# Layer 1's output projection: five token tiles begun beside the last four attention heads, and the last pair's rows in one load

## The chip, the cores and the metric

The kernel runs on one core of a Trainium2 chip. Five engines work side by side, each through its own instructions in a fixed order: TensorE (PE: matrix products into PSUM), VectorE (DVE), ScalarE (ACT), GpSimd (POOL) and SyncE (SP, which here issues every DMA). The metric is the device time of one execution in microseconds (us), the median of several. Lower is better.

## What is computed

Two decoder layers over 1024 tokens of width 1024, and a final RMSNorm. Layer 0 mixes by forgetting attention, layer 1 by native sparse attention (NSA). The part that matters here is the end of layer 1: sixteen heads of width 64 make `o`, `o` is gated, and then the output projection, the residual and the norm follow.

```python
def reference(x, norm_g, fox_w_in, ..., nsa_w_out, final_g):
    for i in range(DEPTH):
        h = rmsnorm(x, norm_g[i])
        ...
        x = x + y
    return rmsnorm(x, final_g)

def nsa_mixer(h, ...):
    ...
    o = g[..., 0:1] * o_c + g[..., 1:2] * o_s + g[..., 2:3] * o_w
    return (o.reshape(B, S, W) * jax.nn.silu(z)) @ w_out
```

`o_s` is attention over chosen blocks, `o_w` over a window of 512 tokens, `o_c` over compressed blocks. `z` is a projection of `h` of the same width as `o`.

## The kernel before

**Precision.** A float32 product is made of three: each operand is split into a high part `hi` (ACT copies it) and a low part `lo` (the difference, by DVE or POOL), and `mm3` (lines 133 to 135) issues hi·hi, hi·lo and lo·hi into one PSUM sum. One such group of three has 128 channels of `o` (one value of k, eight in all), 128 tokens and 512 output columns.

**The head stage of layer 1.** `run_attn` goes through 32 half-heads: head `h` from 0 to 15, for each the later 512 tokens (`s` = 1) and then the earlier ones (`s` = 0). While the products with V of one half-head run (`O_n`, lines 1315 to 1317, after the transposes `ptp_n` on line 1307), the scores of the next are made (`S_n`, line 1275; DVE masks them and finds the extremum on line 1282, ACT takes the exponential on line 1285, POOL splits it on lines 1288 and 1289, and a transposing DMA brings it to `hT`). `finish` (lines 1347 to 1351) ends a half-head: DVE writes `u`, POOL adds it into `ot`. After the second head of a pair, `close` transposes `ot` (`ptn_n`, line 1364), DVE and POOL apply scale and gate, and SP writes 128 rows of `oF` in DRAM. Pair 7 (heads 14 and 15) writes the last 128 of the 1024 rows.

**The filler.** `merge` puts other work between the steps of the heads: for every unit of head cost that is recorded, so much filler (`ratio`, here 0.36). The filler is `nsa_zs`: eight projections `z` (48 products each, `nz`), and after each half of the last one the loading and splitting of four 128-row parts of the output weights `wo` (`load_wout`: SP loads float32 rows into `lo`, ACT copies them to `hi`, line 536, DVE subtracts, line 537). Where a generator yields a function, the filler waits until it returns true. A scheduler then orders each engine's instructions by what it expects to be ready; the order is fixed before the run.

**The output stage.** `out_layer` takes eight tiles of 128 tokens in the order 4, 5, 6, 7, 0, 1, 2, 3. For each: load the tile of `oF` into `of` (line 696), split it into `ohi` and `olo` (lines 697 and 698), make 48 products (two halves of 512 columns, eight k), load the residual `xr`, add (line 727), square and sum, and scale by the norm (line 106), and write the result out. For tiles 4 and 5, seven of the eight k are issued ahead of the loop (`early`). All of it stands behind the head stage in the program.

**Buffers.** In the head stage PSUM has two banks for `O_n`, `nz` and the like (`ps_a`), two pairs of banks for scores (`ps_s2`) and two for transposes. `out_tiles` shares its buffers with the weights of the `z` projections: one `wst` tile for what is loaded, two pairs `whi`, `wlo` for the split. K and V of head group 2 (heads 8 to 11) lie in the pool `kv[0]`, those of group 3 in the pool `at`.

Of the kernel before, what the change touches and what calls it, by code (L numbers as in the profile page):

```python
# [8 lines left out]
F32 = mybir.dt.float32  # L9
# [26 lines left out]
def f(ap):  # L36
    return ap.bitcast(F32)
# [3 lines left out]
def tile_fox_nsa(ctx, tc, a, out):  # L41
# [20 lines left out]
    def ps_a(name):  # L62
        return psA.tile([P, 512], F32, tag="A", name=name)
# [451 lines left out]
    def out_tiles(name):  # L515
        return wp.tile([P, KC, P], F32, tag="wst", bufs=1, name=f"of{name}"), *out_parts(name)
# [6 lines left out]
    def load_wout(pool, i, half):  # L523

        hi, lo = (pool.tile([P, 4, D], F32R, tag=f"h{half}{x}", name=f"wo{i}_{half}_{x}") for x in range(2))
        for k in range(4):
            r = 4 * (1 - half) + k
            dma(f(lo[:, k, :]), wD[i][r * P:(r + 1) * P, :])
        if i:
            yield 2000  # L530
        for k in range(4):
            for c in range(2):
                if i:
                    yield 400
                cs = slice(c * 512, c * 512 + 512)
                A.copy(hi[:, k, cs], f(lo[:, k, cs]))
                (V if i else G).tensor_tensor(lo[:, k, cs], f(lo[:, k, cs]), f(hi[:, k, cs]), OP.subtract)
# [138 lines left out]
    sa.release()  # L676


    def out_layer(ow, w, src, res, g, after, name, early=()):

        gB = ow.tile([P, D], F32, name=f"gB{name}")
        dma(gB, g.to_broadcast([P, D]))
        pend, first = [], list(ready.get("ys", {}))
        bufs = 4 if first else 2
        cs = [slice(half * 512, half * 512 + 512) for half in range(2)]

        def tiles(t):
            if not early:
                return out_tiles(f"{name}_{t}")
            of = ow.tile([P, KC, P], F32, tag="of", bufs=3, name=f"of{name}_{t}")  # L690
            return of, *out_parts(f"{name}_{t}")

        def products(t, tile, ys, ks):
            of, oh, ol = tile
            c = slice(ks[0], ks[-1] + 1)
            dma(of[:, c, :], src[:, t * P:(t + 1) * P].rearrange("(k p) t -> p k t", p=P)[:, c, :])
            A.copy(oh[:, c, :], of[:, c, :])  # L697
            V.tensor_tensor(ol[:, c, :], of[:, c, :], f(oh[:, c, :]), OP.subtract)  # L698
            for half, ts in enumerate(cs):
                if len(ys) <= half:  # L700
                    ys.append(ps_a(f"y{name}_{t}_{half}"))
                for k in ks:
                    wh, wl = w[k // 4]
                    mm3(ys[half], oh[:, k, :], ol[:, k, :], wh[:, k % 4, ts], wl[:, k % 4, ts], k == 0, k == KC - 1)

        begun = {}
        for t in early:
            ps = ps_s2(f"y{name}_{t}")
            begun[t] = tiles(t), [ps[:, half, :] for half in range(2)]
            for ks in (range(0, 4), range(4, 7)):  # L710
                products(t, *begun[t], ks)
        for t in (4, 5, 6, 7, 0, 1, 2, 3):
            tk = slice(t * P, (t + 1) * P)
            ys = ready.get("ys", {}).pop(t, [])
            steps = () if ys else (range(0, 4), range(4, KC)) if t == 4 else (range(KC),)
            xt = ow.tile([P, D], F32, tag="x", bufs=bufs, name=f"xr{name}_{t}")
            nm = Norm(ow, xt, f"n{name}_{t}", bufs)
            if t in begun:
                tile, ys = begun.pop(t)
                steps = (range(7, 8),)  # L720
            elif not ys:
                tile = tiles(t)
            for ks in steps:
                products(t, tile, ys, ks)
            dma(xt, res[tk, :])
            for ps, ts in zip(ys, cs):
                V.tensor_tensor(xt[:, ts], ps, xt[:, ts], OP.add)  # L727
# [495 lines left out]
    class NsaSuper:  # L1223
# [30 lines left out]
        def unit(self, y, qi):  # L1254
# [100 lines left out]
        def close(self):  # L1355
# [9 lines left out]
            V.scalar_tensor_tensor(o, pt, vinv[:, self.g:self.g + 1], o, OP.mult, OP.add)  # L1365
            G.tensor_tensor(o, o, ready["z", p, s][s], OP.mult)
            dma(oF[p * P:(p + 1) * P, s * 512:(s + 1) * 512], o)
            yield 450
# [6 lines left out]
    fo = tc.alloc_tile_pool(name="fo", bufs=1, reuse_waits="tile")  # L1375
    def after1(t, xt, h):
        for c in (slice(0, 512), slice(512, D)):
            dma(out[t * P:(t + 1) * P, c], h[:, c])
# [104 lines left out]
```

## Time and profile before

| | |
|---|---|
| median of 3 runs | 1527.96 us (1526.06 to 1528.8) |
| profiled execution | 1529.59 us, of which 1527.8 us from the first to the last instruction |
| mean granted TensorE clock | 0.974 |
| busy share of PE, DVE, ACT, POOL | 93%, 70%, 53%, 37% |
| chain that ended last, share by engine | PE 63%, DVE 16%, ACT 8%, DMA 6%, issue 4% |
| matrix products | 10488, each with one weight load |

Times in the views count from the span's start. A window view lists, for a stretch of the span, the busy time of each engine with the number of instructions that touch the stretch, then the granted TensorE clock (PEclk), the mean busy share of the 16 DMA engines and GB/s. A busy PE is not PE at its peak: products overlap, and the time from one start to the next is what counts. PEld is the weight loads. In a chain, each row is a piece of the work that ended last, with its start and length.

### The profile page before, as it was taken

How to read it: one execution, taken by the hardware profiler on the slowest of the kernel's cores; microseconds unless marked ns; L12 is line 12 of the kernel's file. 1: busy time of each engine (PE TensorE's matmuls, PEld its weight loads, DVE VectorE, ACT ScalarE, POOL GpSimd, SP SyncE). 2: the span in 40 equal slices, each digit the busy share in tenths (PEclk: the TensorE clock that was granted, in tenths of full speed). 3: DMA queues.
4: the chain of work that ended last, by engine and by line, in shares of the span. 5: the costliest groups of instructions: out<-in, count | busy, mean ns of one | idle time of the engine just before them, and what ended most of it. 6: DMA issues, size and time to landing. Idle time of an engine off the chain costs nothing.

```text
span 1527.8 us, 29541 instructions
## 1 busy us (share of the span) xinstructions
PE 1421.9 (93%) x10488; PEld 1179.8 (77%) x10488; DVE 1066.2 (70%) x2759; ACT 805.1 (53%) x2028; POOL 565.1 (37%) x604
## 2 busy tenths in 40 slices
PE   5999999999999778999999899999999999988698
PEld 4888888888788556878888777778888888876576
DVE  6586878788787864457554668677888788888143
ACT  5364646646565652224131664476767676676031
POOL 1232222222322600033333332366767766575000
PEclk9999999999999979999999998999999999999799
DMA  7796777866777765342435577586777857766442
GB/s 254 238 180 142 163 158 157 182 153 143 172 165 166 178 124 197 121 136 83 156 98 163 148 187 201 180 184 133 180 152 146 204 124 144 189 142 147 132 151 83
DMA packets 405812, 242.72 MB, mean 159 GB/s; under 512 B 332513, under 2 KB 353889, under 8 KB 405409
## 3 DMA queue, kind: packets, MB, share of 16 engines
q1 hardware_dynamic: 405664, 240.84, 64.8%
q8 instruction: 83, 1.36, 0.4%
q14 instruction: 65, 0.52, 0.1%
HBM read 120.96 MB, written 44.11 MB: 108 GB/s over the span
## 4 chain that ended last, share of the span: by engine, by line
PE 63%; DVE 16%; ACT 8%; DMA 6%; issue 4%; POOL 1%; SPq 1%; POOLq 0%; DVEq 0%; ACTq 0%
PE S_n L1275 5%; PE y L133 3%; PE y L135 3%; PE y L134 3%; PE ptp_n L1307 3%; ACT P_n L1285 2%; DVE P_n L1282 2%; PE v L133 2%; PE v L135 2%; PE v L134 2%; DVE hl L605 2%; PE S L585 2%; ACT P L603 2%; PE k L133 2%; PE k L134 2%
## 5 line engine op out<-in xcount | busy, mean ns | idle before, releaser
L1285 ACT ACTIVATE P_n<-P_n,m_n 128x640 f32<-128x640 f32 (+7 forms) x256 | 187.2, 732 | 68.5 <-DVE m_n L1282 34.4
L1275 PE MATMUL S_n<-nk,nq 128*128 128x320 f32 (+5 forms) x768 | 180.0, 350 | 8.6 <-DVE m_n L1282 8.3
L603 ACT ACTIVATE P<-P,m 128x512 f32<-128x512 f32 (+1 forms) x192 | 116.9, 610 | 131.4 <-DVE m L594 130.7
L574 POOL TENSOR_TENSOR Bd<-B,tri 128x128 f32<-128x128 f32 x128 | 62.3, 502 | 245.8 <-DVE m L594 227.5
L1289 POOL TENSOR_TENSOR hl_n<-P_n,hl_n 128x640 f16<-128x640 f32 (+4 forms) x128 | 145.0, 1133 | 9.8
L1275 PEld LDWEIGHTS S_n<-nk,nq 128*128 128x128 f32 x768 | 125.2, 193 | 20.9 <-DVE m_n L1282 10.8
L605 DVE SCALAR_TENSOR_TENSOR hl<-P,hl 128x512 f16<-128x512 f32 (+1 forms) x192 | 124.6, 667 | 20.5 <-ACT hl L604 19.5
L1282 DVE CUSTOM_DVE_ANT_0 P_n<-S_n,wmask 128x640 f32<-128x640 f32 (+2 forms) x192 | 113.4, 595 | 25.7 <-PE S_n L1275 16.0
L1288 POOL CAST hl_n<-P_n 128x640 f16<-128x640 f32 (+4 forms) x128 | 77.0, 601 | 122.1 <-ACT P_n L1285 107.8
L150 ACT ACTIVATE pth_n<-ptp_n 128x512 f16<-128x512 f32 (+1 forms) x160 | 85.9, 547 | 49.9 <-PE ptp_n L1307 48.8
L133 PE MATMUL y<-wo,ohi 128*128 128x512 f32 x240 | 97.5, 406 | 15.4 <-ACT ohi L697 13.9
L151 DVE SCALAR_TENSOR_TENSOR ptl_n<-ptp_n,pth_n 128x512 f16<-128x512 f32 (+1 forms) x160 | 99.9, 632 | 15.4 <-ACT pth_n L150 13.9
L1307 PE MATMUL ptp_n<-ident,P_n 128*128 128x128 f32 x576 | 92.4, 281 | 9.4 <-DVE ptl_n L151 4.3
L135 PE MATMUL y<-wo,olo 128*128 128x512 f32 x240 | 95.9, 402 | 0.8 <-DVE olo L698 0.8
L134 PE MATMUL y<-wo,ohi 128*128 128x512 f32 x240 | 96.0, 400 | 0.0
L604 ACT ACTIVATE hl<-P 128x512 f16<-128x512 f32 (+1 forms) x192 | 92.5, 513 | 4.5 <-DMA pT<-hl 3.1
L1307 PEld LDWEIGHTS ptp_n<-ident,P_n 128*128 128x128 f32 x576 | 66.9, 143 | 20.8 <-DVE ptl_n L151 9.5
L585 PE MATMUL S<-KH,Q 128*128 128x512 f32 (+1 forms) x192 | 68.1, 368 | 11.3 <-DVE m L594 10.9
L1315 PE MATMUL O_n<-nv,pth_n 128*128 128x64 f16 x576 | 72.0, 196 | 6.5 <-ACT pth_n L150 5.5
L727 DVE TENSOR_TENSOR xr<-y,xr 128x512 f32<-128x512 f32 x32 | 21.5, 689 | 73.5 <-PE y L135 65.6
L1315 PEld LDWEIGHTS <-pth_n 128*128 128x128 f16 x576 | 52.2, 98 | 25.3 <-ACT pth_n L150 11.1
L1316 PE MATMUL O_n<-nv,pth_n 128*128 128x64 f16 x576 | 71.0, 194 | 0.0
(384 smaller groups left out, 4566.0 us busy)
## 6 DMA issues: line engine op xcount, KB each, us to landing
nq<-qD SPq DMA_DIRECT2D x64, 256.0 KB
B<-cD SPq DMA_DIRECT2D x16, 512.0 KB
wo<-wD SPq DMA_DIRECT2D x16, 512.0 KB
nq<-qD SPq DMA_DIRECT2D x64, 128.0 KB
of<-oF SPq DMA_DIRECT2D x11, 512.0 KB
x<-in_x_dram SPq DMA_DIRECT2D x8, 512.0 KB
wst_k<-in_fox_w_dram SPq DMA_DIRECT2D x8, 512.0 KB
wst_v<-in_fox_w_dram SPq DMA_DIRECT2D x8, 512.0 KB
```

Of the source, the lines that this page charges most:

```text
L133: T.matmul(ps, wh, mh, start=first, stop=False, **kw)
L134: T.matmul(ps, wh, ml, start=False, stop=False, **kw)
L135: T.matmul(ps, wl, mh, start=False, stop=last, **kw)
L151: V.scalar_tensor_tensor(lo[:, 0:n], pt[:, 0:n], scale, h, OP.mult, OP.subtract)
L603: A.activation(L[:, 0:n], L[:, 0:n], AF.Exp, bias=init, scale=-1.0, accum_out=self.lr[:, col + c:col + c + 1])
L605: V.scalar_tensor_tensor(lo[:, cs], L[:, 0:n], UP, hi[:, cs], OP.mult, OP.subtract)
L1275: T.matmul(ps[:, b, 0:w], self.q[x][:, qi * P:(qi + 1) * P], k[:, k0 + b * w:k0 + b * w + w], start=(x == 0), stop=(x == 1))
L1282: V.tensor_tensor_reduce(dst, src, mk, 1.0, 3e38, OP.add, OP.min, m)
L1285: A.activation(L, L, AF.Exp, bias=m, scale=-1.0, accum_out=self.l[:, y, qi:qi + 1])
L1289: G.tensor_tensor(hl[:, n:2 * n], L, hl[:, 0:n], OP.subtract)
L1307: T.transpose(pt[:, (x + i) * P:(x + i + 1) * P], L[:, kb * P - k0:(kb + 1) * P - k0], ident)
L1315: T.matmul(o, hi, v[:, 0:64], start=first, stop=False)
```

## The change

- `out_start` is new filler behind the last `z` projection. It makes products of the output projection from rows of `oF` that are already written: for tiles 4, 5 and 6 first k = 0 to 3, then k = 4 to 6, and for tiles 7 and 0 k = 0 to 6 in one piece.
- The sums of tiles 4, 5 and 6 are taken out of PSUM after each piece: their residual rows are loaded early into the space of K and V of head group 2 (`xs1`), and DVE adds each piece there. Tiles 7 and 0 keep their sums in the two pairs of score banks (`ys1`), and so wait until the last scores are made (`"scores"`).
- From super 24 on (head 12, later half) the filler's ratio is 0.62; before that it is 0.35 and not 0.36.
- The loads of the output weights' first half are issued ahead of the second half of the last `z` projection; their split, and all of the second half, come after it. Half of the subtractions of the split go to POOL.
- Behind the heads, `out_rest` loads the last pair's 128 rows of `oF` for all tokens (in two halves, `l7`), splits them once, and makes the products of k = 7 for the five begun tiles from them (6 each). Tiles 1, 2 and 3 are made whole as before. Layer 0's call of `out_layer` is left with the parts that it used.

```diff
-    def run_attn(supers, lead, late):
+    def run_attn(supers, lead, late, ratios):
...
         for n, sup in enumerate(supers):
+            if n in ratios:
+                yield (ratios[n],)
...
         if i:
-            yield 2000
+            yield 0
...
-                (V if i else G).tensor_tensor(lo[:, k, cs], f(lo[:, k, cs]), f(hi[:, k, cs]), OP.subtract)
+                (V if i and c else G).tensor_tensor(lo[:, k, cs], f(lo[:, k, cs]), f(hi[:, k, cs]), OP.subtract)
...
         w = next_w(("z", 7))
-        for half in (1, 0):
-            yield from nsa_z(7, w, (half,))
-            yield from load_wout(h1, 1, half)
+        yield from nsa_z(7, w, (1,))
+        rows0 = load_wout(h1, 1, 1)
+        yield next(rows0)
+        yield from nsa_z(7, w, (0,))
+        yield from rows0
+        yield from out_start(load_wout(h1, 1, 0))
+    def out_start(rows1):
+        yield next(rows1)
+        yield lambda: ("done", 5) in ready
+        kv0 = kv[0]
+        for t in (4, 5):
+            xs1[t] = kv0.tile([P, D], F32, tag=f"k{t - 4}", name=f"xr1_{t}")
+        xs1[6] = Halves(*(kv0.tile([P, 512], F32, tag=f"v{y}", name=f"xr1_6_{y}") for y in range(2)))
+        for t in (4, 5, 6):
+            for cs in cols2:
+                dma(xs1[t][:, cs], x1[t * P:(t + 1) * P, cs])
+        parts = [(t, 0, 4) for t in (4, 5, 6)] + [(t, 4, 7) for t in (4, 5, 6)] + [(t, 0, 7) for t in (7, 0)]
...
+        def met(n):
+            t, _, stop = parts[n]
+            return ("o", stop - 1, t // 4) in ready and (4 <= t <= 6 or "scores" in ready)
...
+        for n, (t, k0, stop) in enumerate(parts):
+            if n == 2:
+                yield from rows1
+            more = n + 1 < len(parts)
+            soon = more and met(n + 1)
+            if t not in xs1:
+                ps = ps_s2(f"y1_{t}")
+                ys1[t] = [ps[:, half, :] for half in range(2)]
+            for half in range(2):
+                if soon:
+                    (load, split)[half](n + 1)
+                _, oh, ol = pend[n]
+                pt = ps_a(f"y1_{t}_{k0}_{half}") if t in xs1 else ys1[t][half]
+                yield from products(pt, ready["wout"], oh, ol, half, range(k0, stop), t in xs1)
+                if t in xs1:
+                    V.tensor_tensor(xs1[t][:, cols2[half]], pt, xs1[t][:, cols2[half]], OP.add)
...
-    merge(run_attn([NsaSuper(h, s) for h in range(H) for s in (1, 0)], 0.8, 3), filler, 0.36, cap=1400)
+    merge(run_attn([NsaSuper(h, s) for h in range(H) for s in (1, 0)], 0.8, 3, {24: 0.62}), filler, 0.35, cap=1400)
...
+    def out_rest(w):
...
+        lh, ll = out_parts("1_r7")
+        l7 = f(ll.rearrange("p k t -> p (k t)"))
+        for half in (1, 0):
+            dma(l7[:, cols2[half]], oF[7 * P:8 * P, cols2[half]])
+            c = slice(4 * half, 4 * half + 4)
+            A.copy(lh[:, c, :], f(ll[:, c, :]))
+            V.tensor_tensor(ll[:, c, :], f(ll[:, c, :]), f(lh[:, c, :]), OP.subtract)
+        for t in (4, 5, 6, 7, 0, 1, 2, 3):
...
+                if t in (1, 2, 3):
+                    for _ in products(pt, w, oh, ol, half, range(KC), True):
+                        pass
+                else:
+                    wh, wl = w[1]
+                    mm3(pt, lh[:, t, :], ll[:, t, :], wh[:, 3, cs], wl[:, 3, cs], t not in ys1, True)
```

How the built order moves shows at three places. The first is PE at the start of head 14, beside the end of head 13: scores `S_n14` and transposes `ptp_n13`, in the order before.

```order
L1275 MATMUL S_n14_1_1_0_17800<-nk_3_1_16438,nq0_14_1_17771 128x320
L1275 MATMUL S_n14_1_1_0_17800<-nk_3_1_16438,nq1_14_1_17772 128x320
L1307 MATMUL ptp_n13_0_1_17818<-ident_72,P_n13_0_0_1_17540 128x128
L1307 MATMUL ptp_n13_0_1_17818<-ident_72,P_n13_0_0_2_17591 128x128
L1307 MATMUL ptp_n13_0_1_17818<-ident_72,P_n13_0_0_3_17652 128x128 x2
L1275 MATMUL S_n14_1_0_1_17827<-nk_3_0_16434,nq0_14_1_17771 128x384
L1275 MATMUL S_n14_1_0_1_17827<-nk_3_0_16434,nq1_14_1_17772 128x384
```

The same place of PE in the order of the change; `y1_4_0_0` is token tile 4, k from 0, columns 0 to 511.

```order
L1331 MATMUL S_n14_1_1_0_17858<-nk_3_1_16438,nq0_14_1_17821 128x320
L1331 MATMUL S_n14_1_1_0_17858<-nk_3_1_16438,nq1_14_1_17822 128x320
L133 MATMUL y1_4_0_0_17845<-wo1_1_0_17230,ohi1_4_0_17711 128x512
L134 MATMUL y1_4_0_0_17845<-wo1_1_1_17231,ohi1_4_0_17711 128x512
L135 MATMUL y1_4_0_0_17845<-wo1_1_0_17230,olo1_4_0_17712 128x512
L1363 MATMUL ptp_n13_0_1_17875<-ident_72,P_n13_0_0_1_17570 128x128
L1363 MATMUL ptp_n13_0_1_17875<-ident_72,P_n13_0_0_2_17623 128x128
L1363 MATMUL ptp_n13_0_1_17875<-ident_72,P_n13_0_0_3_17688 128x128 x2
L1331 MATMUL S_n14_1_0_1_17884<-nk_3_0_16434,nq0_14_1_17821 128x384
```

A group of three products now stands between scores and transposes. Counted over the whole order, 90 products of the output projection stand ahead of the last product with V: 24 each of tiles 4, 5 and 6 (k = 0 to 3) and 18 of tile 4 (k = 4 to 6); the `z` projections have the same 48 in heads 12 to 15 as before.

The second place is PE behind the last product with V (`O_n15_0`), in the order before; `ptn_n15_0` is the last pair's transpose.

```order
L1317 MATMUL O_n15_0_18826<-nv_3_1_16440,hT_n15_0_18509 128x64
L1364 MATMUL ptn_n15_0_18900<-ident_72,ot_n14_0_18497 128x128 x4
L133 MATMUL y1_4_18915<-wo1_1_0_17311,ohi1_4_18917 128x512
L134 MATMUL y1_4_18915<-wo1_1_1_17312,ohi1_4_18917 128x512
L135 MATMUL y1_4_18915<-wo1_1_0_17311,olo1_4_18918 128x512
```

The same place of PE in the order of the change.

```order
L1373 MATMUL O_n15_0_18965<-nv_3_1_16440,hT_n15_0_18617 128x64
L133 MATMUL y1_5_4_0_19058<-wo1_0_0_17694,ohi1_5_4_18825 128x512
L134 MATMUL y1_5_4_0_19058<-wo1_0_1_17695,ohi1_5_4_18825 128x512
L135 MATMUL y1_5_4_0_19058<-wo1_0_0_17694,olo1_5_4_18826 128x512
...
L1420 MATMUL ptn_n15_0_19045<-ident_72,ot_n14_0_18605 128x128 x4
...
L133 MATMUL y1_6_4_0_19086<-wo1_0_0_17694,ohi1_6_4_19055 128x512
...
L133 MATMUL y1_7_19110<-wo1_1_0_17230,ohi1_7_0_19083 128x512
```

Before, 384 products stand behind the last product with V, and all of them behind the last transpose. Now 294 do: 18 of tile 5 (six ahead of the transpose) and 18 of tile 6, 42 each of tiles 7 and 0, then 30 of k = 7 and 144 of tiles 1, 2 and 3.

The third place is the end of SP's order, whose DMAs are issued one behind the other, before.

```order
L1291 DMA_TRANSPOSE hT_n15_0_18509<-hl_n15_0_1_3_18729 128x8x128
L1367 DMA oF_82<-no_7_1_17776 128x512
L1367 DMA oF_82<-no_7_0_17991 128x512
L682 DMA gB1_18913<-in_final_g_dram 128x1024
L696 DMA of1_4_18916<-oF_82 128x4x128
L696 DMA of1_4_18916<-oF_82 128x3x128
L696 DMA of1_5_18968<-oF_82 128x4x128
```

The same end of SP's order in the change.

```order
L1223 DMA of1_6_4_19054<-oF_82 128x3x128
L1347 DMA_TRANSPOSE hT_n15_0_18617<-hl_n15_0_1_3_18855 128x8x128
L1423 DMA oF_82<-no_7_1_17826 128x512
L1223 DMA of1_7_0_19082<-oF_82 128x7x128
L1423 DMA oF_82<-no_7_0_18061 128x512
L1436 DMA gB1_19206<-in_final_g_dram 128x1024
L1223 DMA of1_0_0_19111<-oF_82 128x7x128
L1448 DMA xr1_7_19279<-x1_83 128x1024
L1448 DMA xr1_0_19300<-x1_83 128x1024
L1448 DMA xr1_1_19321<-x1_83 128x1024
L1451 DMA of1_1_19323<-oF_82 128x8x128
L1440 DMA olo1_r7_19209<-oF_82 128x512 x2
```

Before, every load of `oF` for the output stage is issued behind the write of the last rows (`no_7_0`). Now all but tile 0's and those of `out_rest` are issued ahead of it.

More of the change, by code (lines that the diff above doesn't have):

```diff
@@ L676, in tile_fox_nsa, with products, out_layer @@
     sa.release()
-    def out_layer(ow, w, src, res, g, after, name, early=()):
+    cols2 = [slice(half * 512, half * 512 + 512) for half in range(2)]
+    def products(ps, w, oh, ol, half, ks, last):
+        for k in ks:
+            wh, wl = w[k // 4]
+            mm3(ps, oh[:, k, :], ol[:, k, :], wh[:, k % 4, cols2[half]], wl[:, k % 4, cols2[half]],
+                k == ks[0], last and k == ks[-1])
+            yield 650
+    def out_layer(ow, w, src, res, g, after, name):
         gB = ow.tile([P, D], F32, name=f"gB{name}")
@@ L682, in out_layer @@
         dma(gB, g.to_broadcast([P, D]))
[L683 to L711, printed above, removed]
+        pend, first = [], list(ready["ys"])
         for t in (4, 5, 6, 7, 0, 1, 2, 3):
             tk = slice(t * P, (t + 1) * P)
[L714 to L724, printed above, removed]
+            ys = ready["ys"].pop(t, [])
+            xt = ow.tile([P, D], F32, tag="x", bufs=4, name=f"xr{name}_{t}")
+            nm = Norm(ow, xt, f"n{name}_{t}", 4)
+            if not ys:
+                of, oh, ol = out_tiles(f"{name}_{t}")
+                dma(of, src[:, tk].rearrange("(k p) t -> p k t", p=P))
+                A.copy(oh, of)
+                V.tensor_tensor(ol, of, f(oh), OP.subtract)
+                for half in range(2):
+                    ys.append(ps_a(f"y{name}_{t}_{half}"))
+                    for _ in products(ys[half], w, oh, ol, half, range(KC), True):
+                        pass
@@ L725, in out_layer @@
             dma(xt, res[tk, :])
-            for ps, ts in zip(ys, cs):
+            for ps, ts in zip(ys, cols2):
                 V.tensor_tensor(xt[:, ts], ps, xt[:, ts], OP.add)
@@ L1198, in nsa_zs, with __init__, __getitem__ @@
         w = next_w(("z", 7))
[L1199 to L1201 removed]
+        yield from nsa_z(7, w, (1,))
[4 more added lines that the diff above has]
+        yield from out_start(load_wout(h1, 1, 0))
+    class Halves:
+        def __init__(self, *x):
+            self.x = x
+        def __getitem__(self, key):
+            return self.x[key[1].start // 512]
@@ new lines, in tile_fox_nsa, with load, split @@
+    xs1, ys1 = {}, {}
+    def out_start(rows1):
[9 more added lines that the diff above has]
+        parts = [(t, 0, 4) for t in (4, 5, 6)] + [(t, 4, 7) for t in (4, 5, 6)] + [(t, 0, 7) for t in (7, 0)]
+        pend = {}
+        def met(n):
+            t, _, stop = parts[n]
+            return ("o", stop - 1, t // 4) in ready and (4 <= t <= 6 or "scores" in ready)
+        def load(n):
+            t, k, stop = parts[n]
+            pend[n] = out_tiles(f"1_{t}_{k}")
+            dma(pend[n][0][:, k:stop, :], oF[k * P:stop * P, t * P:(t + 1) * P].rearrange("(k p) t -> p k t", p=P))
+        def split(n):
+            _, k, stop = parts[n]
+            of, oh, ol = (x[:, k:stop, :] for x in pend[n])
+            A.copy(oh, of)
+            V.tensor_tensor(ol, of, f(oh), OP.subtract)
+        yield lambda: met(0)
+        load(0)
+        yield 2000
+        split(0)
+        for n, (t, k0, stop) in enumerate(parts):
[6 more added lines that the diff above has]
+                ys1[t] = [ps[:, half, :] for half in range(2)]
+            for half in range(2):
+                if soon:
[5 more added lines that the diff above has]
+                    V.tensor_tensor(xs1[t][:, cols2[half]], pt, xs1[t][:, cols2[half]], OP.add)
+            if more and not soon:
+                yield lambda n=n: met(n + 1)
+                load(n + 1)
+                yield 1000
+                split(n + 1)
@@ L1271, in unit @@
             w = n if n <= 512 else n // 2
+            if (h, s, y, qi) == (H - 1, 0, 1, 3):
+                ready["scores"] = True
             c = 0
@@ L1367, in close @@
             dma(oF[p * P:(p + 1) * P, s * 512:(s + 1) * 512], o)
+            ready["o", p, s] = True
             yield 450
-    merge(run_attn([NsaSuper(h, s) for h in range(H) for s in (1, 0)], 0.8, 3), filler, 0.36, cap=1400)
+    merge(run_attn([NsaSuper(h, s) for h in range(H) for s in (1, 0)], 0.8, 3, {24: 0.62}), filler, 0.35, cap=1400)
     at.release()
-    kv[0].release()
[L1375 to L1378, printed above, removed]
```

26 lines of the change are left out of this document (24 added, 2 removed).

## The prediction

> **What bounds the kernel now.** I read the view by windows first, cut where the stages of layer 1 end. Columns: start and end, length, then PE, PEld, DVE, ACT and POOL with busy us and number of instructions, PEclk, DMA share, GB/s. The first two rows are heads 8–9 and 10–11, then 12–13 and 14–15, the gap behind the last product with V, the output stage's products, and the rest.
>
> ```profile
> 1204.00:1255.70 51.70, 50.23 (x626) 43.23 (x621) 42.67 (x118) 35.90 (x86) 34.80 (x40) 1.00 0.70 149
> 1255.70:1307.20 51.50, 50.20 (x625) 43.22 (x622) 42.02 (x117) 35.90 (x86) 34.92 (x43) 1.00 0.71 139
> 1307.20:1365.60 58.40, 52.78 (x624) 45.04 (x619) 49.39 (x131) 40.77 (x98) 36.93 (x42) 0.94 0.74 169
> 1365.60:1416.90 51.30, 40.98 (x553) 35.20 (x552) 39.18 (x106) 33.71 (x81) 30.10 (x34) 0.93 0.66 154
> 1416.90:1429.20 12.30, 1.40 (x10) 0.84 (x7) 1.49 (x3) 0.62 (x1) 1.98 (x2) 0.50 0.54 139
> 1429.20:1521.00 91.80, 90.05 (x384) 73.35 (x384) 31.70 (x56) 21.77 (x49) 0.00 (x0) 0.98 0.38 122
> 1521.00:1527.80 6.80, 0.00 (x0) 0.00 (x0) 2.40 (x5) 1.02 (x3) 0.00 (x0) 0.86 0.20 77
> ```
>
> PE sets the pace in heads 8 to 11 (97% busy) and in the output stage (98%). Heads 12 to 15 have PE idle for 5.6 and 10.3 us, and then comes a hole of 12 us. The same view of the `z` products alone gives the filler of each pair of heads: 48 in a loaded pair, 36 and 12 in the last two.
>
> ```profile
> 1204.00:1255.70 51.70, 15.02 (x49) 8.21 (x49) 1.37 (x2) 1.18 (x2) 2.54 (x3) 1.00 0.70 149
> 1255.70:1307.20 51.50, 15.04 (x48) 8.20 (x48) 1.38 (x2) 1.18 (x2) 2.52 (x3) 1.00 0.71 139
> 1307.20:1365.60 58.40, 11.99 (x36) 6.36 (x36) 0.69 (x1) 0.60 (x1) 3.62 (x3) 0.94 0.74 169
> 1365.60:1416.90 51.30, 4.02 (x12) 2.10 (x12) 0.69 (x1) 0.60 (x1) 2.54 (x2) 0.93 0.66 154
> ```
>
> Then the chain that ended last shows what the hole is and what a product costs, row by row: start, length, piece.
>
> ```profile
> 1417.25 0.70 DVE u_n L1350
> 1418.02 0.72 POOL ot_n L1351
> 1418.74 2.00 issue
> 1420.74 1.31 POOLq L1479
> 1422.92 5.56 DMA of<-oF
> 1428.50 0.63 ACT ohi L697
> 1429.17 0.80 PE y L133
> ...
> 1430.39 0.43 PE y L135
> ...
> 1440.02 0.23 PE y L134
> ...
> 1459.57 5.74 DMA xr<-x
> 1465.40 0.70 DVE xr L727
> ...
> 1520.97 0.70 DVE xr L727
> ```
>
> The last head is finished and gated on DVE and POOL, only then SP loads the first tile of `oF`, and the products begin at 1429.17. SP's own rows say why the load is late: it sits in front of the last write for 7 us.
>
> ```profile
> 1415.30 7.09 SPq L1367 DMA_DIRECT2D oF<-no  x2
> 1422.92 2.96 SPq L696 DMA_DIRECT2D of<-oF  x5
> ```
>
> The first products are 0.43 us apart, later ones 0.23: PE comes out of the hole at half clock (PEclk 0.50 in the window). A stretch without waits gives the pitch.
>
> ```profile
> 1470.00:1490.00 20.00, 20.00 (x90) 16.57 (x89) 7.60 (x12) 5.10 (x11) 0.00 (x0) 1.00 0.39 132
> ```
>
> 90 products touch 20 us, two of them only at its edges: 20 / 88 = 0.227 us.
>
> **The output stage after the change.** From the last head's `u` (1417.25) to the end today: 1527.8 − 1417.25 = 110.55 us. By the order, 294 of 384 products are left behind that point, and they start there: 294 × 0.227 = 66.7. The four transposes among them take less than the 1.4 us that PE is busy in the hole today; I take 0.6. From the last product to the end nothing changes: 1527.8 − 1520.97 = 6.8. New waits are possible at three places, for `ohi` and `olo` of tiles 7, 0 and 1. Tile 7's load stands ahead of the last write. Issued when the last head ends, and at the chain's 5.56 us for a load, it lands near 1423; a split takes up to 2 × 0.62 us on ACT and 1.22 on DVE (rows below), so 8.0 us in all, against 36 products of tiles 5 and 6 (8.2 us). Tile 0's load waits until tile 7 is split, and has tile 7's 42 products (9.5 us) as cover for the same 8.0. The last rows' load waits for tile 7's buffer and has tile 0's 42. So the cover suffices by 0 to 1.5 us each time. If a load takes twice as long, each place shows about 5 us; I take 2 for all three, between 0 and 15. Sum: 66.7 + 0.6 + 6.8 + 2 = 76.1, a gain of **34.4**. It contains the hole (11.9 less the 0.6), the slow clock behind it, the part of the wait for `xr` (5.74 us of DMA in the chain) that stopped PE, and 90 × 0.227 = 20.4 of products that moved.
>
> **The heads after the change.** Heads 12 to 15 take 58.4 + 51.3 = 109.7 now with 48 filler products. They will have 138. A loaded pair takes 51.6 with 48, so two take 103.2 with 96; 42 more at pitch cost 9.5: 112.7, or **+3.0**. This is the rate of heads without the stalls of today's last four. Those stalls are seen in ACT's rows: the copy of `wo` waits for its load, and the exponentials behind it on ACT wait too.
>
> ```profile
> 1332.27 1.14 ACT L536 CAST wo<-wo 128x512 fp32r<-128x512 f32 x2 [2.56 <-DMA wo<-wD]
> 1381.27 0.62 ACT L536 CAST wo<-wo 128x512 fp32r<-128x512 f32 x1 [2.44 <-DMA wo<-wD]
> 1384.66 1.14 ACT L536 CAST wo<-wo 128x512 fp32r<-128x512 f32 x2 [1.55 <-DMA wo<-wD]
> ```
>
> Against the loaded rate (51.6 less 0.227 for each filler product that is missing), heads 12–13 lose 58.4 − 48.9 = 9.5 and heads 14–15 lose 51.3 − 43.4 = 7.9. The change issues the first loads ahead of the second half of `z7`, so 24 products (5.4 us) stand beside them; but the copies still come on ACT soon after the loads. The bounds are none of the loss kept (+3.0) and all of it (3.0 + 17.4 = **+20.4**, every moved product paid in full). Below +3.0 the bound is −6.5: all 42 extra products go into gaps, and four heads take 103.2. I take half of the 6.55 us that the three waits for `wo` had, as they are the nearest rows: **+6.3**. The last wait, for the transposed probabilities of the last half-head, stays, and products of tile 4 fill it.
>
> ```profile
> 1416.49 0.20 PE L1315 MATMUL O_n<-nv,hT_n 128*128 128x64 f16 x1 [2.33 <-DMA hT_n<-hl_n]
> ```
>
> **Other engines.** An add of a partial sum, a split of four k and a subtraction of `wo` cost:
>
> ```profile
> L727 DVE TENSOR_TENSOR xr<-y,xr 128x512 f32<-128x512 f32 x16 | 10.9, 690 | 53.6 <-PE y L135 49.4 <-DMA xr<-x 4.3
> L698 DVE TENSOR_TENSOR olo<-of,ohi 128x512 fp32r<-128x512 f32 x2 | 1.4, 692 | 8.8 <-ACT ohi L697 8.8
> L697 ACT CAST ohi<-of 128x512 fp32r<-128x512 f32 x2 | 1.2, 618 | 16.1 <-DMA of<-oF 16.1
> L698 DVE TENSOR_TENSOR olo<-of,ohi 128x1024 fp32r<-128x1024 f32 x6 | 7.3, 1223 | 1.7 <-ACT ohi L697 1.7
> L537 POOL TENSOR_TENSOR wo<-wo,wo x16: 1267/1290/1740, 494.7 to 525.6; 128x512 fp32r<-128x512 f32 x16
> L537 DVE TENSOR_TENSOR wo<-wo,wo x16: 635/686/1869, 1333.8 to 1408.1; 128x512 fp32r<-128x512 f32 x16
> ```
>
> Into the heads go eight adds (5.5 us of DVE) and five splits (3.5 DVE, 3.1 ACT); eight subtractions (5.5) leave DVE for POOL (10.3, the price of layer 0's rows). DVE then has 88.6 + 3.5 = 92 us of about 116, ACT 77.6, POOL 77.3: each under the 83% that DVE has in a loaded pair, so I cost them at nothing; that cover is gone if an instruction waits at the head of such a queue (below). Four more adds in the output stage lie on DVE, 35% busy there. The loads of `x1` stand on SP ahead of transposes and wait for K and V of group 2, whose last reader, head 11, is done by then; 1.5 MB at a DMA share of 0.74 I cost at nothing too. The ratio 0.35 for 0.36 moves a few products within a pair; the two loaded pairs differ by 0.2 us, so ±1.2 for six pairs, taken as 0.
>
> GPSIMD Engine Reference (section Specifications) in the Trainium skill says that GpSimd shares its SBUF interfaces with VectorE and contends with DVE instructions that have two SBUF inputs: a rule against the eight subtractions on POOL. The rows bear it out in part: the subtraction on DVE has a median of 686 ns and a largest of 1869 beside POOL's work. If each of the eight costs DVE that difference, the sum below is worse by 8 × 1.18 = 9.4 us, an estimate; by the median rows it is unchanged.
>
> **The sum.** The profiled execution has 1529.59 us (1.8 outside its span); 1529.59 − 34.4 + 6.3 = 1501.5. The median shown is 1.6 lower, so **1500 us**.
>
> **The rivals.**
> *The heads swallow the filler.* PEld is 84% in loaded heads, so PE may have 16% free; for it speaks the idle PE of heads 12 to 15, against it that PEld is also 83% in the stretch of pure products, where PE has no gap at all. The heads would take 103.2 us: 1500 − 6.3 − 6.5 = 1487. Perfetto Trace Analysis (section Identifying the Most-Contended Engine) in the Trainium skill takes LDWEIGHTS busy share, not matmul busy, as the measure of PE's headroom; by it this rival would be likely, and the stretch of pure products disagrees. Chance 0.10.
> *The loads of the output stage lie open.* One `wst` buffer chains load, split and products of tiles 7, 0 and the last rows; for it speaks that the cover is so thin, against it that each load has nearly the cover that it needs. Two of the three exposed with their split cost 2 × 8.0 = 16.0, less the 2 taken: 1514. Chance 0.15.
> *The adds block DVE.* In the heads each of eight adds stands in DVE's order ahead of the maxima of the next scores (line 1282), and waits until its 12 products, dealt out between head steps, are done. While DVE waits, score banks stay full and PE stops. In the output stage an add waits 53.6 / 16 = 3.35 us on average. Eight such waits cost 26.8: 1527, no change. From 28 / 8 = 3.5 us each the kernel is slower; at 24 products' time (5.45 us) it is 1500 + 43.6 = **1544**. For it: the groups of three are spread over half a head. Against it: in DVE's order the first add stands behind a split of `ptp` whose transpose PE makes beside the add's last products. Chance 0.08, of which 0.05 on the slower side.
> My forecast has the remaining 0.67.
>
> **How the numbers follow.** The heads' bounds (−6.5 to +20.4, about +6.3) give 1487 to 1514, and this range takes in the first rival and most of the second: about 0.85 of the chance, the inner cases not all at their ends. About 0.2% (3 us) is what a measurement of this kernel can tell from no change. Faster by more: 0.67 + 0.10 + 0.15, less 0.01 for the unforeseen, 0.91; within it 0.04; slower 0.05.
>
> **What would show it.** Right: the first `y` of tile 5, k = 4 to 6 starts within 1 us of the last product with V; no half clock behind it; from there to the end about 76 us; heads 12 to 15 between 113 and 120. Wrong: PE waits above 3 us for `ohi` of tiles 7, 0 or 1 (second rival); DVE idle before the adds in the heads, released by PE (third); heads 12 to 15 at 130 us or more, by waits for `wo` or `hT`.

## The result and the profile after

The changed kernel takes 1502.03 us (median of 4 runs, 1497.71 to 1504.16) against 1527.2 us before (4 runs beside them, 1526.06 to 1528.8): a ratio of 0.9829, 95% interval 0.9811 to 0.9846. The profiled execution took 1503.75 us, 1502.0 of it the span.

The view by windows of the changed kernel, cut at the same points as that of before: heads 8–9, 10–11, 12–13 and 14–15, then the output stage from the last product with V to the last product of all, then the rest.

```profile
1203.20:1254.80 51.60, 50.48 (x626) 43.20 (x623) 42.37 (x118) 36.25 (x86) 34.32 (x40) 1.00 0.81 155
1254.80:1306.30 51.50, 50.20 (x627) 43.34 (x624) 42.31 (x122) 37.52 (x89) 35.96 (x44) 1.00 0.74 165
1306.30:1376.60 70.30, 62.68 (x658) 52.83 (x655) 54.12 (x131) 46.63 (x110) 47.95 (x50) 0.93 0.79 186
1376.60:1427.10 50.50, 49.27 (x612) 41.27 (x608) 38.82 (x105) 30.39 (x74) 26.60 (x33) 1.00 0.64 115
1427.10:1495.20 68.10, 67.84 (x305) 55.39 (x300) 32.69 (x58) 19.36 (x45) 2.23 (x3) 1.00 0.45 153
1495.20:1502.00 6.80, 0.15 (x1) 0.00 (x0) 2.43 (x5) 1.02 (x3) 0.00 (x0) 0.77 0.20 77
```

Behind the last product with V there were 12.3 + 91.8 + 6.8 = 110.9 us; there are 74.9 now, 36.0 fewer. The window with PE at 1.4 us of 12.3 is gone, and so is the half clock. Heads 12 to 15 grew from 109.7 to 120.8 us, 11.1 more. Up to head 11 the profile is 0.9 us shorter. −36.0 + 11.1 − 0.9 = −25.8, which is the difference of the spans.

The growth isn't even. Heads 14–15 hold 66 products of the projection and keep PE 98% busy at full clock. Heads 12–13 have PE idle for 7.6 us at a clock of 0.93; the loaded pairs above idle for 1.1 and 1.3 us at 1.00.

Behind the last product with V the products go on at once. PE's rows there (start, length of one) and SP's rows:

```profile
1427.09 0.19 PE L1373 MATMUL O_n<-nv,hT_n 128*128 128x64 f16 x1
1427.26 0.50 PE L133 MATMUL y<-wo,ohi 128*128 128x512 f32 x1
```

```profile
1427.77 0.37 SPq L1223 DMA_DIRECT2D of<-oF  x1
1432.03 0.33 SPq L1423 DMA_DIRECT2D oF<-no  x1
```

Tile 7's load is issued at 1427.77, ahead of the last write at 1432.03, and PE waits for neither: its only wait in the whole stage is 0.3 us for the last head's output.

```profile
PE ptn_n L1420 <- POOL ot_n L1407: 0.3, 1, 0.3
```

Where PE stops in heads 12 and 13 is seen in its waits there (total, times, longest) and in the chain of waits, which follows the first stop back to a load of `wo` and the second to SP:

```profile
PE S_n L1331 <- DMA nq<-qD: 3.0, 2, 2.3
PE S_n L1331 <- DVE m_n L1338: 3.0, 3, 2.1
```

```profile
1324.37 3.52 DMA wo<-wD
...
1327.91 1.15 ACT wo L538 x2
...
1329.08 1.34 DVE wo L539
1330.42 0.73 DVE P_n L1338
...
1331.22 1.38 PE S_n L1331 x4
1332.60 0.43 PE nz L133
...
1348.98 1.28 POOL wo L539
1350.26 0.23 POOL hl_n L1344
...
1352.61 1.21 SPq L1347
...
1353.87 0.58 SPq L1032
...
1355.00 4.91 DMA nq<-qD
...
1360.05 1.14 PE S_n L1331 x3
1361.18 0.43 PE y L135
```

**First stop** (2.1 us, up to 1331.2): the scheduler put ACT's copies of `wo` right behind their loads; ACT waits 3.05 us for the load, DVE subtracts, and only then finds a row maximum whose score bank PE needs. **Second stop** (0.7 and 2.3 us, up to 1360.0): POOL subtracts a part of `wo` ahead of a cast of probabilities, SP waits for the cast to issue its transpose, and the queries of head 14 stand behind that transpose and behind the second block's loads of `wo`:

```profile
1342.34 0.64 SPq L530 DMA_DIRECT2D wo<-wD  x1
1345.13 1.33 SPq L1347 DMA_TRANSPOSE hT_n<-hl_n  x1
1346.51 1.17 SPq L530 DMA_DIRECT2D wo<-wD  x2
1348.86 1.35 SPq L1347 DMA_TRANSPOSE hT_n<-hl_n  x1
1350.26 0.67 SPq L530 DMA_DIRECT2D wo<-wD  x1
1351.04 2.78 SPq L1347 DMA_TRANSPOSE hT_n<-hl_n  x2
1353.87 0.58 SPq L1032 DMA_DIRECT2D nq<-qD  x1
```

Behind both stops the next products are 0.43 us apart, where they are 0.23 elsewhere: half the clock.

### The profile page after: what moved, and what is told of

It reads as the page before. It is cut to its first block, busy times and chain, and to the rows that moved or that the text cites. A ratio compares the mean times of both kernels' runs of the same rounds, so it can differ in the third digit from the quotient of the medians.

```text
span 1502.0 us, 29578 instructions
## 1 busy us (share of the span) xinstructions
PE 1418.6 (94%) x10488; PEld 1176.0 (78%) x10488; DVE 1069.9 (71%) x2764; ACT 806.4 (54%) x2029; POOL 572.6 (38%) x612
## 4 chain that ended last, share of the span: by engine, by line
PE 67%; DVE 16%; ACT 6%; DMA 5%; issue 4%; POOL 2%; SPq 0%; DVEq 0%; ACTq 0%; POOLq 0%
PE S_n L1331 6%; PE y L133 4%; PE y L135 4%; PE y L134 3%; PE ptp_n L1363 3%; PE v L133 2%; PE v L135 2%; PE v L134 2%; PE S L587 2%; PE S L588 2%; PE k L133 2%; PE O L621 2%; PE k L134 2%; DVE hl L607 2%; PE k L135 2%
## 5 line engine op out<-in xcount | busy, mean ns | idle before, releaser
L1331 PE MATMUL S_n<-nk,nq 128*128 128x320 f32 (+5 forms) x768 | 178.6, 347 | 10.8 <-DVE m_n L1338 7.5
L133 PE MATMUL y<-wo,ohi 128*128 128x512 f32 x230 | 95.4, 415 | 4.5 <-ACT ohi L702 4.5
L135 PE MATMUL y<-wo,olo 128*128 128x512 f32 x230 | 92.6, 404 | 1.0 <-DVE olo L703 1.0
L134 PE MATMUL y<-wo,ohi 128*128 128x512 f32 x230 | 92.8, 404 | 0.0
L1363 PEld LDWEIGHTS ptp_n<-ident,P_n 128*128 128x128 f32 x576 | 66.7, 142 | 18.8 <-DVE ptl_n L151 11.3
L587 PE MATMUL S<-KH,Q 128*128 128x512 f32 (+1 forms) x192 | 68.3, 369 | 10.0 <-DVE m L596 9.8
L1338 DVE CUSTOM_DVE_ANT_0 P_n<-S_n,bias 128x640 f32<-128x640 f32 (+1 forms) x64 | 65.1, 1018 | 9.9 <-PE S_n L1331 9.9
L1371 PE MATMUL O_n<-nv,pth_n 128*128 128x64 f16 x576 | 70.5, 195 | 1.1 <-ACT pth_n L150 0.6
L1372 PE MATMUL O_n<-nv,pth_n 128*128 128x64 f16 x576 | 69.6, 193 | 0.0
L1373 PE MATMUL O_n<-nv,ptl_n 128*128 128x64 f16 x576 | 68.4, 193 | 0.0
```

The source lines that it names most:

```text
L133: T.matmul(ps, wh, mh, start=first, stop=False, **kw)
L134: T.matmul(ps, wh, ml, start=False, stop=False, **kw)
L135: T.matmul(ps, wl, mh, start=False, stop=last, **kw)
L587: T.matmul(ps[:, 0:n], q, KH[j][:, k0:k0 + n], start=True, stop=False)
L1331: T.matmul(ps[:, b, 0:w], self.q[x][:, qi * P:(qi + 1) * P], k[:, k0 + b * w:k0 + b * w + w], start=(x == 0), stop=(x == 1))
L1338: V.tensor_tensor_reduce(dst, src, mk, 1.0, 3e38, OP.add, OP.min, m)
```

## The experiments

Three theories were set against each other for the 11 us of heads 12 to 15. Theory 1: the two stops, one from the splitting of `wo`, one from the late query loads, with half clock behind each. Theory 2: the eight subtractions that went to POOL. Theory 3: these heads carry too much, and a stop that is taken away comes back elsewhere. Two more questions are what a moved product costs, and what tiles 7 and 0 are for.

All edits are made to the changed kernel. The runs came in three groups, each on one chip with the kernel before beside it; before had medians of 1529.95, 1530.37 and 1527.66 us (9 runs each). Ratios are against it. Stage lengths are read from each run's profiled execution, cut at the last product with V of each pair of heads; "output" ends with the last product.

| run | median us | ratio, 95% interval | heads 12–13 | heads 14–15 | output |
|---|---|---|---|---|---|
| changed kernel again | 1501.31 | 0.9815 (0.9792–0.9838) | 70.2 | 50.5 | 68.1 |
| subtractions all on DVE | 1503.07 | 0.9822 (0.9796–0.9848) | 68.4 | 52.1 | 68.1 |
| second block later | 1500.49 | 0.9807 (0.9784–0.9831) | 69.6 | 50.5 | 68.1 |
| gap ahead of the copies | 1500.36 | 0.9811 (0.9787–0.9834) | 66.8 | 50.0 | 69.9 |
| ratio 0.35 throughout | 1507.11 | 0.9849 (0.9827–0.9870) | 58.7 | 54.7 | 80.1 |
| tiles 7 and 0 not begun | 1505.90 | 0.9845 (0.9823–0.9866) | 68.3 | 50.5 | 72.6 |
| no split of `wo` | 1496.91 | 0.9782 (0.9762–0.9803) | 65.1 | 50.3 | 68.1 |
| two loads staged | 1502.49 | 0.9813 (0.9791–0.9835) | 68.5 | 50.5 | 68.1 |
| no split, second block later | 1490.02 | 0.9748 (0.9731–0.9764) | 59.7 | 50.2 | 68.1 |
| two staged, second block later | 1500.17 | 0.9823 (0.9806–0.9839) | 67.3 | 50.5 | 68.1 |
| tile 0 not begun | 1502.67 | 0.9833 (0.9816–0.9849) | 70.5 | 50.6 | 68.7 |
| last rows tile by tile | 1500.34 | 0.9819 (0.9801–0.9836) | 68.7 | 50.5 | 68.1 |

Two things limit what this table can tell. Differences in us below are against the 1501.31 of the first group, and the intervals of the ratio overlap with that kernel's for all rows but "no split, second block later". For the ratio 0.35, tiles 7 and 0 not begun, and no split, all executions do lie outside the eight of the changed kernel (1497.71 to 1504.16). The stage lengths come from one execution each. Three runs change only what stands behind the heads (the two without tiles, and the last rows tile by tile), and PE's and SP's orders in heads 12–13 are those of the changed kernel. With its two profiles these five spread from 68.3 to 70.5 us in heads 12–13 and from 118.8 to 121.1 in heads 12 to 15. A difference of 2 us in these columns shows nothing.

**The changed kernel again.**

> The changed kernel itself once more, so that the other runs have it beside them: 1502 us, within 3 us; heads 12 and 13 take about 70 us with two stops of PE (2.4 and 2.7 us) and half clock behind each.

1501.31 us; the stops are there again, 2.8 and 4.0 us long. Heads 12 to 15 take 120.7 us, within 0.1 of the first profile. Half clock follows only the second stop, not each as expected (last section).

**All subtractions of `wo` on DVE.**

```diff
-                (V if i and c else G).tensor_tensor(lo[:, k, cs], ...
+                (V if i else G).tensor_tensor(lo[:, k, cs], ...
```

> All sixteen subtractions of wo of layer 1 stand on DVE, as before the change. Theory 1 (a chain of stalls: the copies of wo wait for their loads on ACT, and the query loads of head 14 stand on SP behind the second block's loads): the two stops of PE stay, the time is within 3 us of the changed kernel. Theory 2 (the eight subtractions on POOL cost it, by slowing DVE's subtractions to 1.3 to 1.7 us and by standing ahead of POOL's casts): 5 to 9 us faster than the changed kernel. Theory 3 (heads 12 and 13 carry too much, wherever it stands): 0 to 3 us slower, since DVE takes 5.5 us more.

1503.07 us, heads 12 to 15 120.5: no gain, so theory 2 falls; theories 1 and 3 both allow this time. The first half of theory 2 is real in part: groups of line 539 (shortest/median/longest ns) of the changed kernel and, behind it, of this run.

```profile
L539 DVE TENSOR_TENSOR wo<-wo,wo x8: 637/922/1840, 1329.1 to 1362.1; 128x512 fp32r<-128x512 f32 x8
```

```profile
L539 DVE TENSOR_TENSOR wo<-wo,wo x16: 632/684/1660, 1327.6 to 1382.9; 128x512 fp32r<-128x512 f32 x16
```

With POOL subtracting beside it, DVE's median is 922 ns, without 684. That is 1.9 us of DVE for eight, and it didn't reach the time. Not all of it is due to POOL's subtractions of `wo`: the two longest of the eight (1.68 and 1.84 us) ran mostly beside POOL's line 1345, the low part of the probabilities, which both runs have.

**The second block's loads one part later.**

```diff
-        yield next(rows1)
         yield lambda: ("done", 5) in ready
...
+            if n == 1:
+                yield next(rows1)
             if n == 2:
                 yield from rows1
```

> The loads of the second block of wo are issued one part later, so that three of its four loads stand on SP behind the query loads of head 14. Theory 1: the stop at the first scores of head 14 (0.9 + 2.7 us) and the half clock behind it (about 3 us) go, 4 to 7 us faster than the changed kernel; the first stop stays. Theory 2: within 2 us of it, the late cast on POOL still holds the transposes. Theory 3: within 2 us, the stop comes back at the next wait.

The wait for the queries is gone from PE's list, as theory 1 wanted, but the time is within 1 us, as theory 3 had it (and theory 2, which has fallen). PE now waits longer for the row maxima: the row of this run, and the same row of the changed kernel's second profile.

```profile
PE S_n L1332 <- DVE m_n L1339: 6.6, 5, 3.7
```

```profile
PE S_n L1331 <- DVE m_n L1338: 3.9, 3, 2.8
```

Part of this is the split at a new place. The second block's loads now land later, and ACT waits for one of them ahead of exponentials that PE's next transposes need. PE then stops for 1.0, 1.5 and 0.6 us, where in the first profile it had stopped 3.0 us for the queries. ACT's row of this run:

```profile
1356.90 0.62 ACT L538 CAST wo<-wo 128x512 fp32r<-128x512 f32 x1 [1.60 <-DMA wo<-wD]
```

**A gap between the loads and the copies of the first block.**

```diff
-            yield 0
+            yield 2000 if half else 0
```

> 2000 units of filler time with no work stand again between the loads and the copies of the first block of wo (as before the change); by this the loads of the second block fall behind the query loads of head 14 too. Theory 1: both stops of PE and the half clock behind them go, 6 to 11 us faster than the changed kernel; some nine products move from the heads to the output stage at no cost either way. Theory 2: 0 to 2 us faster. Theory 3: within 2 us of it, heads 12 and 13 give back what heads 14 and 15 then take.

1500.36 us. The gap didn't do what it was meant to: the scheduler still put the copies behind the loads, ACT waited 3.6 us and PE stopped for 3.8. The queries no longer stop PE here either, but it waits 6.1 us in all for row maxima. Heads 12 to 15 are 3.9 us shorter with nine products fewer, the output stage is 1.8 longer.

**The ratio left at 0.35.**

```diff
-... 0.8, 3, {24: 0.62}), filler, 0.35, cap=1400)
+... 0.8, 3, {}), filler, 0.35, cap=1400)
```

> The last four heads keep the ratio 0.35, so that 36 instead of 90 products of the output projection stand ahead of the last product with V. Theory 4 (a product costs its pitch of 0.227 us wherever it stands, as long as the hole behind the last head is filled): heads 12 to 15 become 54 x 0.227 = 12.3 us shorter, the output stage as much longer, the time is within 3 us of the changed kernel. Rival (the heads take products into idle time that the output stage has not): the output stage is 12.3 us longer, the heads less than 8 us shorter, 4 to 12 us slower. Other rival (the fast pace through heads 12 and 13 makes the stops): the heads are 16 us shorter or more, 4 us or more faster.

5.8 us slower than the changed kernel in the first group, as the first rival had it. Windows of heads 12–13, 14–15 and the output stage:

```profile
1306.50:1365.20 58.70, 53.86 (x621) 44.80 (x620) 45.30 (x119) 38.26 (x92) 36.12 (x40) 0.94 0.80 183
1365.20:1419.90 54.70, 47.32 (x584) 40.07 (x583) 40.75 (x110) 36.69 (x89) 38.09 (x43) 0.94 0.65 141
1419.90:1500.00 80.10, 79.95 (x352) 65.47 (x352) 37.10 (x65) 20.88 (x48) 2.23 (x3) 1.00 0.41 135
```

With 54 products fewer the heads are 120.7 − 113.4 = 7.3 us shorter, the output stage 12.0 longer. A product costs 0.222 us there and 0.135 in the heads (0.10 to 0.14, by the spread of the heads). PE idles in these heads for 12.2 us and loses about 0.06 × 113.4 = 6.8 to the slow clock; in the changed kernel's second profile it is 10.3 and 3.5 (its clock is 0.95 over 70.2 us). The difference of 5.2 is about what the heads don't give back: part of what is put into them falls into idle and slow time.

**Tiles 7 and 0 not begun, and tile 0 alone not begun.**

```diff
-... + [(t, 0, 7) for t in (7, 0)]
+...
```

> Tiles 7 and 0 are not begun ahead of the last rows; they make their 48 products in the loop. Only what is left of tiles 4 to 6 (54 products, some 9 us behind the last product with V) stands in front of the last pair's rows. If these two tiles are the cover of write, load and split of the last rows (write 1432.0, load about 3 us, split 2 us after it, against 1436.5 for the end of the cover): PE stops 3 to 5 us before the first product with the last rows and runs at half clock behind it, 4 to 8 us slower than the changed kernel. If the three tiles cover it alone: within 2 us. If most of the hole comes back: 10 us slower or more.

4.6 us slower, and the output stage is 4.5 longer. Of the 54 products, 18 are made in the heads, so 36 stand ahead of the last rows. PE stops for them for 1.5 us, less than the 3 to 5 expected, and the products behind the stop are 0.42 apart.

```profile
1433.76 0.39 PE L135 MATMUL y<-wo,olo 128*128 128x512 f32 x1
1435.68 0.50 PE L133 MATMUL y<-wo,ohi_r 128*128 128x512 f32 x1 [1.54 <-ACT ohi_r L1442]
...
1438.46 0.63 PE L133 MATMUL y<-wo,ohi_r 128*128 128x512 f32 x1
1438.88 0.63 PE L134 MATMUL y<-wo,ohi_r 128*128 128x512 f32 x1
```

```diff
-... + [(t, 0, 7) for t in (7, 0)]
+... + [(t, 0, 7) for t in (7,)]
```

> Tile 0 is not begun ahead of the last rows. If the cover for write, load and split of the last rows is what the two tiles are for: 42 products of tile 7 (9.5 us) behind the end of tiles 4 to 6 are enough for the 3 to 5 us that were open without both, the time is within 2 us of the changed kernel. If the order of loads through the one buffer counts (the last rows' load waits for a split to be used up): 2 to 5 us slower.

1502.67 us, the output stage 0.6 longer, no wait of PE for the last rows. One tile of 42 products behind the 36 is cover enough.

**The last rows tile by tile.**

```diff
-        for half in (1, 0):
-            dma(l7[:, cols2[half]], oF[7 * P:8 * P, cols2[half]])
-            c = slice(4 * half, 4 * half + 4)
+        for t in (4, 5, 6, 7, 0):
+            dma(l7[:, t * P:t * P + P], oF[7 * P:8 * P, t * P:t * P + P])
+            c = slice(t, t + 1)
```

> The last pair's rows come tile by tile (five loads of 128x128 and five splits for the five begun tiles), in place of two loads of 512 columns. If the one load is only a smaller number of instructions under the cover of tiles 7 and 0: within 1.5 us of the changed kernel. If each load's way from issue to landing is paid: 3 us slower or more, with PE waiting for ohi of the last rows.

1500.34 us, the output stage 68.1 as before. Under this cover the one load for the last rows is worth nothing that can be measured.

**No splitting of `wo`.**

```diff
                 cs = slice(c * 512, c * 512 + 512)
+                if i:
+                    continue
...
-        ready.setdefault("wout", []).append((hi, lo))
+        ready.setdefault("wout", []).append((lo, lo) if i else (hi, lo))
```

> Leaves out the splitting of wo of layer 1 (sixteen copies on ACT, eight subtractions each on DVE and POOL); the products take the loaded values for both parts, and are as many as before. Theory 1 (copies of wo at the head of ACT's queue wait for their loads, and that makes the first stop of PE): both stops of PE in heads 12 and 13 and the half clock behind them go, heads 12 to 15 take 109 to 114 us, the time is 6 to 12 us below the changed kernel. Theory 3 (heads 12 and 13 stop for another reason, such as transposes and query loads that SP issues late): less than 3 us below it.

4.4 us below the changed kernel, heads 12 to 15 at 115.4: between the two expectations. The first stop is gone (one wait of 1.0 us for row maxima is left, later). The second stayed, at the same place of SP's order. As POOL subtracts nothing of `wo` here, its subtraction ahead of the cast isn't needed for this stop:

```profile
PE S_n L1333 <- DMA nq<-qD: 2.2, 1, 2.2
```

**Two loads of the first block staged in freed K.**

```diff
+        stage = [kv[0].tile([P, D], F32, tag=f"k{k}", ...) for k in range(2)]
+        for k in range(2):
+            dma(stage[k], wD[1][k * P:(k + 1) * P, :])
         yield from nsa_z(7, w, (1,))
-        rows0 = load_wout(h1, 1, 1)
+        rows0 = load_wout(h1, 1, 1, stage)
```

> Two of the four loads of the first block of wo go into the freed K of group 2 ahead of the last z projection, so that ACT has copies whose data is there when the other two loads are issued. Theory 1: ACT's wait for wo (3.1 to 3.8 us) falls to 2 us or less, the first stop of PE goes, 3 to 5 us faster than the changed kernel. Theory 3: the stop moves to the next wait, within 2 us of it.

1502.49 us. ACT does have four copies to make early, but its wait for the other two loads stays near 2.9 us, so the wait itself was hardly shortened, and the run says little of it.

```profile
1329.93 1.14 ACT L540 CAST wo<-wo 128x512 fp32r<-128x512 f32 x2 [2.86 <-DMA wo<-wD]
```

**Both causes gone at once: no splitting, and the second block later.** The edits of the two runs above together.

> Leaves out the splitting of wo of layer 1, and issues the second block's loads one part later, with three of the four behind the query loads of head 14: both known causes of the two stops of PE are gone at once. Theory 1 (the two stops are the whole of what heads 12 and 13 pay too much): no stop above 1 us in heads 12 and 13, heads 12 to 15 take 109 to 112 us, 8 to 11 us below the changed kernel. Theory 3 (PE then stops at the next late step): heads 12 to 15 take 114 us or more, 6 us below it or less.

1490.02 us, ratio 0.9748 (0.9731 to 0.9764). Heads 12–13 and 14–15:

```profile
1301.10:1360.80 59.70, 57.94 (x656) 49.23 (x654) 46.70 (x124) 39.37 (x93) 35.97 (x42) 1.00 0.99 219
1360.80:1411.00 50.20, 49.26 (x606) 41.18 (x605) 38.74 (x106) 30.13 (x73) 26.15 (x32) 1.00 0.65 116
```

109.9 us, the clock at 1.00, no stop above 1.0 us. In the first profile the two stops last 2.1 and 3.0 us, and half clock costs 1.7 and 2.8 more (last section): 9.6 of the 10.9 us that are gone. So theory 1 has about the right size. That the waits alone make the stops isn't shown, as the run leaves out the work of the split too. Theory 3 is right in one thing, that one cause taken away leaves or moves part of the cost: without the late queries heads 12 to 15 were 0.6 us shorter (within the spread), without the split 5.3, without both 10.8.

**Staged, and the second block later.** The edits of those two runs together; the output is complete.

> Two of the first block's loads of wo ahead into the freed K, and the second block's loads one part later; the output is complete. Theory 1: heads 12 to 15 take 114 us or less, 5 to 8 us faster than the changed kernel. Theory 3: 116 to 120 us, 0 to 4 us faster.

1500.17 us, heads 12 to 15 at 117.8. This is in the range of theory 3, 2.9 us below the second profile but only 1.0 below the spread, and the time can't be told from the changed kernel's. ACT still waits 3.0 us for the other two loads. No version that keeps the split was shown to beat the changed kernel.

## Why the prediction was right, step by step

- **The output stage** was put at 76.1 us from the last head's `u`; from `u` at 1427.64 to the end at 1502.0 it takes 74.4. 294 products at the pitch were right: from `u` to the end of the last product (1495.2) it is 67.6 us, put at 66.7 + 0.6. The waits were put at 2 us and came to 0.3. The first product of tile 5 starts 0.2 us behind the last with V, at full clock, as forecast. The gain is 36.2 in place of 34.4. The chain's row of `u`:

```profile
1427.64 0.69 DVE u_n L1406
```

- **The cover of the loads** was thought to suffice by 0 to 1.5 us. The split of tile 7 ended 1.8 us ahead of its first product (1434.7 against 1436.5), tile 0's 4.7, the last rows' 4.6:

```profile
1433.63 1.09 DVE L1229 TENSOR_TENSOR olo<-of,ohi 128x896 fp32r<-128x896 f32 x1 [0.30 <-ACT ohi L1228]
...
1440.21 1.09 DVE L1229 TENSOR_TENSOR olo<-of,ohi 128x896 fp32r<-128x896 f32 x1 [2.80 <-ACT ohi L1228]
1449.63 1.32 DVE L1443 TENSOR_TENSOR olo_r<-olo_r,ohi_r 128x512 fp32r<-128x512 f32 x2 [8.32 <-ACT ohi_r L1442]
```

  The rival of loads that lie open fell with it; that it was a rival at all is shown by the run without tiles 7 and 0.
- **The heads** were the weak step: +6.3 forecast, +11.1 measured, within the bounds; their 120.8 us lie just above the 113 to 120 that were named as a sign. Two terms of it were mis-sized, against each other. Heads without the stops were put at 112.7 us; the run without both causes took 109.9, 2.8 less. (It has no splitting either, so this is a lower end.) A loaded pair was the wrong measure for heads 14–15, which hold no scores of a next head: 612 PE instructions with 66 products, against 626 with 48. And "half of the 6.55 us" for the stops, 3.3, was too little: the stops, with the split's work, take 120.8 − 109.9 = 10.9. The forecast counted the waits for `wo` on ACT; it had neither the queries, which the new order sets behind the second block's loads on SP, nor the half clock behind each stop.
- **Other engines at no cost**: right for the eight subtractions (all on DVE gave nothing). The estimate of 9.4 us, made from the longest row, didn't come about. GPSIMD Engine Reference (section Specifications) in the Trainium skill names contention with DVE instructions that have two SBUF inputs. The rows agree, at 0.24 us in the median of a subtraction.
- **The adds that block DVE**: in heads 13 to 15 DVE waited 0.9 us in all for products ahead of such adds. This rival fell.

```profile
DVE xr L1250 <- PE y L135: 0.9, 2, 0.6
```

- **Heads that swallow the filler**: in small part. The four heads grew, but a product there cost some 0.135 us in place of 0.227.
- The sum, 1501.5 for the profiled execution, met 1503.75: heads +4.8, output −1.8, heads 0 to 11 −0.9. That it is so close is in part luck: the heads' two errors (−2.8 and +7.6) and the output stage's stand against each other.

What stays open: whether the split's cost is ACT's wait for the load or the work of the copies and subtractions. The run that was to shorten the wait alone didn't shorten it.

## What to carry to other kernels

Filling a serial gap with work from the other side of a stage boundary paid in full here, because the work needs nothing that the gap produces; the rest of two tiles and the 42 products of one more were cover enough. What such a change brings with it (earlier loads and splits, in queues that the busy stage uses too) is where it is paid: look in each engine's order for what now stands behind a load that isn't there yet. Of two stops in a row, taking away one can show little, as its cost may come back at the next; take away both before a theory of stops is given up.

## What was not expected of the hardware

Half clock behind short stops. The half-heads with the two stops (the second halves of heads 12 and 13):

```profile
1325.50:1342.80 17.30, 15.22 (x129) 13.24 (x124) 13.94 (x26) 11.31 (x24) 12.26 (x12) 0.90 0.69 195
1356.50:1376.60 20.10, 17.14 (x135) 14.48 (x132) 14.19 (x31) 10.75 (x23) 13.86 (x13) 0.83 0.65 123
```

A clock of 0.90 over 17.3 us is 17.3 × 0.10 / 0.5 = 3.5 us at half speed, 0.83 over 20.1 us is 6.8. The first costs half of that, 1.7 us. Of the second, 1.2 us lie in the stop itself, so it costs 2.8. TensorE: Matmul & The Clock Gate (section Part 1: The HAM clock gate) in the Trainium skill has the clock set by free-running windows of about 3.4 us, and half clock after an idle window. The two lengths are about one and two windows, which agrees; but the stops are shorter than a window.

The cost isn't fixed by a stop's length: behind the first stop of the second profile, 2.8 us, there is no half clock. In each profile all changes of the clock lie on a grid of 3.41 us. The first two rows are two steps of this grid in the changed kernel's first profile, the other two are from its second.

```profile
1328.16:1331.57 3.41, 1.33 (x10) 1.09 (x9) 2.48 (x4) 2.44 (x6) 2.96 (x3) 1.00 0.87 236
1331.57:1334.98 3.41, 3.41 (x12) 3.12 (x11) 3.17 (x8) 3.41 (x9) 2.13 (x3) 0.50 1.11 350
```

```profile
1326.64:1330.05 3.41, 1.81 (x12) 1.43 (x10) 0.96 (x1) 1.38 (x3) 1.44 (x2) 1.00 0.96 305
1330.05:1333.47 3.42, 2.25 (x12) 2.11 (x13) 3.42 (x9) 3.40 (x8) 2.34 (x3) 1.00 1.17 282
```

In the first profile 2.1 us of idle time fall into one step, and the next runs at 0.50. In the second the longer stop is shared by two steps, 1.6 and 1.2 us, and the clock stays at 1.00. Over all fourteen profiles, PE was idle for 2.1 us or more in 92 of the steps at full clock, and half clock followed each of them. It followed 61 of the 153 steps with 1.2 to 2.1 us, and none with less. So in these traces a window needn't be wholly idle for half clock, and where a stop lies in the grid bears on its cost.

And a spread ahead of the change: head 12 begins between 1301.1 and 1308.2 us in the profiles of the changed kernel and its variants, whose edits all lie behind that point. That is as much as most effects sought here, so the experiments were read by the lengths of stages.
